# Decay and beta columns carried by the neighbourhood values' weights, values early and gates late

## The chip, the cores and the metric

The kernel runs on one core of one Trainium2 chip. The metric is the device time of one execution in microseconds (us). Beside it stands one profiled execution, from which all stretches, waits and durations are read. Engines are named as in the profile: PE is the tensor engine (matmuls), PEld its weight load, DVE the vector engine, ACT the scalar engine, POOL the GpSimd engine, and SP the engine whose queue issues nearly all DMA transfers.

## The reference

One layer of a hybrid backbone, on 1024 latent tokens and 256 context tokens of width 1024. Modulation vectors come from `silu(c) @ w_ada`. Tokens are normalised and modulated, and one projection `@ w_in` gives all columns:

```python
px = modulate(rms_norm(x, norm1_w[i]), sh1, sc1) @ w_in[i]
pc = modulate(rms_norm(ctx, norm1_w[i]), csh1, csc1) @ w_in[i]
```

- Group A, gated DeltaNet, four heads of 128, forward and backward: q, k, v go through a short convolution and SiLU; `z` (512 columns) gives the output gate `silu(z)`; 16 columns give the decay (`a`) and the strength (`b`) per head and direction. Chunks of tokens need the inverse of a triangular matrix built from k, decay and beta, and then a scan over the chunks with a state per head. The context is scanned first.
- Group B, neighbourhood attention, eight heads of 64: each latent query attends to a window of latent keys and to all context keys.

Both outputs go through one projection, a gated residual, and a SwiGLU feed-forward. Only the latent stream is returned, so the gate `z` is needed for the 1024 latent tokens alone, the decay and beta columns and the values of group B for all 1280.

## The kernel before, in words

Tokens are cut into ten tiles of 128 (two of context, eight latent). The normalised input is held transposed in eight K-slices as a pair of rounded parts, `hh` and `hl`; each weight is split in the same way by ACT (rounded part) and POOL (remainder), and each product is three matmuls per K-slice (line 389 for blocks, line 572 for wide jobs).

The projection is a list `jobs`, run in order by the loop over `n`:

- A `Block` computes 128 columns for all tokens with the weight stationary, in segments of 256, 512 and 512 tokens. Kinds are k, q, v (convolution and SiLU behind it) and nk, nq (keys and queries of group B, with their norm). Its `evac`, `silu`, `norm` and `finish` come in the following jobs.
- A `Wide` job computes half of z or half of group B's values (nv) with the tokens stationary, one tile at a time, 24 matmuls per tile. Its weights come in two loads of 132 columns (z) or 128 (nv). The 16 decay and beta columns stand at the end of z's weights: z's second half computes 248 columns of z and these 16, and, for the two context tiles, only these 16. They go to the tile `ab`.

The order before is: k0, k1, k2, k3, z second half, nk0 to nk2, z first half, nk3, nq0 to nq2, q0 to q3, nv first half, v0, nv second half, v1, v2, v3, nq3.

Beside the jobs run background generators, a few steps per tile or per K-slice: the modulation of the later parts (`modulation`, weights `wad`), then, from the job after the fifth on, `block_inverses` and `preps`. `block_inverses` starts from `ab` (`decay_tables`), runs a long chain on DVE (lines 825 and 827), transposes the result on PE (line 837) and stores it as `x_d`. `preps` makes, for each chunk and direction, a corrected matrix: it loads `kk`, `xc` and, for latent chunks, `at` (lines 872 to 877), takes an Exp on ACT (line 901), matmuls on PE (lines 897 to 920) with sums on DVE (lines 903 and 921), and stores `at_d` and `y_d` (line 930). The latent chunks start only when all q blocks are done. A wide job steps the background by 2 per tile before `turn` and by 5 behind it, a block by 1 and by 3 per K-slice.

All values of a half are stored to memory (`nv_d`); behind the job numbered `values`, sixteen copies from memory to memory (line 1024) cut them into the windows' blocks (`vw_d`). When all `preps` are done, `attention` starts its loads on SP, and behind the last block the scan starts, with the attention as its filling.

The order in which each engine's queue gets its instructions is made by a planner from the program's order and its own estimate of durations; each engine then works strictly in that order. SP's queue is in order too: a transfer that waits holds all that stand behind it. Buffers come from rings: two for `zt` (wide results on their way to memory), three shared under the tag `kx` (kTh, kk, kd, vt, hl16), three for `at`, four banks of PSUM for `blk` behind the fifth job, eight before.

Of the kernel before, what the change touches and what calls it, by code (L numbers as in the profile page):

```python
# [9 lines left out]
F32 = mybir.dt.float32  # L10
# [3 lines left out]
AF = mybir.ActivationFunctionType  # L14
# [22 lines left out]
def const_arrays():  # L37
    p = np.arange(128)[:, None]
    f = np.arange(128)[None, :]
    same = (p // 32) == (f // 32)  # L40
    m = [p == f, p <= f, p >= f, p > f, p < f, (p > f) & same, (p < f) & same]
    big = np.stack([x.astype(np.float32) for x in m[:3] + [(p // 64) == (f // 64)]], 1)
    f32 = np.arange(32)[None, :]
    q = p % 32
    small = np.stack([x.astype(np.float32) for x in
                      [q <= f32, q >= f32, q < f32, q > f32]], 1)
    out = np.concatenate([big.reshape(128, -1), small.reshape(128, -1)], 1)
    masks = np.stack([x.astype(np.float32) for x in m[3:]], 1)
    return np.ascontiguousarray(out), np.ascontiguousarray(masks)
# [38 lines left out]
def hybrid(ctx, tc, a, dbg):  # L88
    nc = tc.nc
    pe, act, dve, pool, sp = nc.tensor, nc.scalar, nc.vector, nc.gpsimd, nc.sync  # L90

    def pools(stack, name, side=None, bufs=1, **kw):
        if side:
            kw["side"] = side
        return stack.enter_context(tc.tile_pool(name=name, bufs=bufs, reuse_waits="tile", **kw))
# [19 lines left out]
    def const(name, shape, dt=F32):  # L115
        return mid.tile(shape, dt, name=name, tag=name)
# [26 lines left out]
    z_d = dram.tile([L, 512], F32, name="z_d", tag="z_d")  # L143
# [4 lines left out]
    nv_d = dram.tile([T, 512], F32, name="nv_d", tag="nv_d")  # L148
# [14 lines left out]
    ab = const("ab", [128, NCH, 16])  # L163
# [196 lines left out]
    with ExitStack() as bs:  # L360
# [7 lines left out]
        def bank(name="m"):  # L368

            if len(psum) == 1:  # L370
                return psum[0].tile([128, 512], F32, name=name, tag="ps")
            return psum[1].tile([128, 512], F32, name=name, tag=name, bufs=4 if name == "blk" else 2)
# [19 lines left out]
        class Block:  # L392


            def __init__(self, kind, i):
                self.kind, self.i = kind, i
                self.segs = SEGS[1:] if kind in ("q", "nq") else SEGS
                self.t0 = self.segs[0][0]
# [149 lines left out]
        class Wide:  # L548


            def __init__(self, kind, half, zp):
                self.kind, self.half, self.zp = kind, half, zp
                self.n = 264 if kind == "z" else 256

            def prefetch(self):
                h2, n = 2 * self.half, self.n // 2
# [19 lines left out]
            def tiles(self):  # L576
                half = self.half
                if self.kind == "nv":
                    for t in range(NCH):
                        p = self.wide(t, 0, 256)  # L580
                        vt = cp.tile([128, 264], F32, name="zt", tag="zt", bufs=2)
                        act.copy(vt[:, :256], p[:, :256])
                        sp.dma_start(nv_d[t * 128:(t + 1) * 128, half * 256:half * 256 + 256], vt[:, :256])
                        yield
                    return
                if half == 1:
                    for t in range(2):
                        p = self.wide(t, 248, 264)
                        act.copy(ab[:, t], p[:, :16])
                    yield  # L590
                nz = 264 if half == 0 else 248
                for t in range(2, NCH):
                    p = self.wide(t, 0, 264)
                    zt = cp.tile([128, 264], F32, name="zt", tag="zt", bufs=2)
                    act.activation(zt[:, :nz], p[:, :nz], AF.Silu)
                    if half:
                        act.copy(ab[:, t], p[:, 248:264])
                    sp.dma_start(z_d[(t - 2) * 128:(t - 1) * 128, half * 264:half * 264 + nz], zt[:, :nz])
                    yield


        first = [Block("k", 0), Block("k", 1)]
        with ExitStack() as xs:
# [67 lines left out]
            for s0, n in SEGS:  # L671
                p = bank()
# [7 lines left out]
            for k in range(KT):  # L680
# [3 lines left out]
                t = xt[k]  # L684
# [16 lines left out]
        cp = pools(bs, "cp", "right")  # L701
# [248 lines left out]
                    live = nxt  # L950
                flush(tick[0] + 2)

        jobs = first + [Block("k", 2), Block("k", 3), Wide("z", 1, zp)]
        inv = len(jobs)
        jobs += [Block("nk", i) for i in range(3)] + [Wide("z", 0, zp), Block("nk", 3)]
        jobs += [Block("nq", i) for i in range(3)] + [Block("q", 0)]
        turn = len(jobs)
        jobs += [Block("q", i) for i in (1, 2, 3)]
        later = len(jobs)
        values = later + 2  # L960
        queries = range(turn - 1, later)
        jobs += [Wide("nv", 0, zp), Block("v", 0), Wide("nv", 1, zp), Block("v", 1), Block("v", 2), Block("v", 3), Block("nq", 3)]

        def blk(n):
            return jobs[n] if 0 <= n < len(jobs) and isinstance(jobs[n], Block) else None
# [351 lines left out]
    with ExitStack() as os_:  # L1317
# [25 lines left out]
        for b in range(KT - 2):  # L1343
            w, nxt = nxt, load_w(a["w_out"][b + 1], lo_engine=dve)
# [38 lines left out]
    with ExitStack() as us:  # L1383
# [66 lines left out]
        for f in range(PLAIN):  # L1450
            po = [[bank(), bank()] for _ in range(2)]
            g = prev[f]
            w = [up.next(), None]
# [103 lines left out]
    for n, (wn, xn) in enumerate(zip(Stream.DOWN, FACTORS)):  # L1557
        o = chains[n in (1, 3, 5)]
        for p in range(NFB // 2):
            w = up.next(1)[0]  # L1560
# [19 lines left out]
def host(inputs):  # L1580
    f = lambda n: np.asarray(inputs[n])
    c = np.ascontiguousarray
    o = {}
    o["cst"], o["masks"] = const_arrays()
    o["c2"] = c(np.stack([f("c")[0].reshape(8, 128), f("c_ctx").reshape(8, 128)], -1).transpose(1, 0, 2))
    o["prm"] = c(np.concatenate([f("norm1_w")[0].reshape(8, 128), f("norm2_w")[0].reshape(8, 128),
                                 f("b_ada")[0].reshape(48, 128)], 0).T)
    o["cw"] = c(f("dn_conv_w")[0].reshape(5, 12, 128).transpose(2, 1, 0))
    o["qkw"] = c(np.stack([np.tile(f("na_q_norm_w")[0], 2), np.tile(f("na_k_norm_w")[0], 2)], -1))
    o["onw"] = c(f("dn_out_norm_w").reshape(128, 1))  # L1590
    o["adt"] = c(np.concatenate([f("dn_A_log")[0].reshape(1, 8), f("dn_dt_bias")[0].reshape(1, 8)], 1))
    xc = np.concatenate([f("ctx")[0], f("x")[0]], 0)
    o["xcT"] = c(xc.T.reshape(8, 128, T))
    wada = f("w_ada")[0]
    o["wa1"] = c(wada[:, :2048].reshape(8, 128, 4, 512).transpose(2, 1, 0, 3)[[2, 0, 3, 1]])
    o["wa2"] = c(wada[:, 2048:].reshape(8, 128, 8, 512).transpose(2, 1, 0, 3))
    w = f("w_in")[0]

    def blocks(w, n=128):
        return c(w.reshape(w.shape[0] // 128, 128, w.shape[1] // n, n).transpose(2, 1, 0, 3))  # L1600

    o["w_conv"] = blocks(w[:, :1536])
    o["w_z"] = blocks(w[:, 1536:2064], 132)
    o["w_nqk"] = blocks(w[:, 2064:3088])
    o["w_nv"] = blocks(w[:, 3088:3600])
    o["w_out"] = blocks(f("w_out")[0])
    gu = np.stack(np.split(blocks(f("w_ffn_in")[0]), 2, 0), 1)
    o["w_gu"] = c(gu.reshape(NFB, 2, 128, 2, 4, 128).transpose(0, 1, 3, 2, 4, 5))
    fo = blocks(f("w_ffn_out")[0]).reshape(2, 4, 128, NFB // 2, 2, 128)
    o["w_fo"] = c(fo.transpose(3, 0, 4, 2, 1, 5))  # L1610
    tab = np.concatenate([f("na_rpb")[0].reshape(8, 465), np.full((8, 1), -1.0e30, np.float32)], 1)
    o["rpb"] = c(tab[:, bias_index()])
    return o


def bias_index():

    idx = np.empty((2, 3, 128, 384), np.int64)
    pad = 15 * 31
    for half in range(2):  # L1620
        for case, cb in enumerate((0, 1, 3)):
            q = np.arange(128)
            r, cq = (half * 8 + q // 16)[:, None], (cb * 16 + q % 16)[:, None]
            k = np.arange(384)
            kr, kc = (half * 4 + k // 32)[None, :], (BLKS[cb] + k % 32)[None, :]
            r0 = np.clip(r - 4, 0, 8)
            w0 = np.clip(cq - 8, 0, 48)
# [19 lines left out]
```

## Time and profile before

| what | value |
|---|---|
| runs | 1632.72, 1635.08, 1635.48 us (median 1635.08) |
| profiled execution | span 1634.2 us; a time of its own beside the span is not given |
| PE busy | 1525.4 us (93%) |
| DVE busy | 1037.2 us (63%) |
| ACT busy | 705.7 us (43%) |
| POOL busy | 203.0 us (12%) |
| traffic | 275.23 MB, 168 GB/s on the mean of the span |
| granted clock of PE, mean | 0.971 |

In rows of windows, each engine's busy time and its count of instructions stand first, then the granted clock (PEclk, 1.00 is full), the busy share of the sixteen DMA engines, and GB/s. In rows of the timeline: start, duration, engine, line, operation, tile written and tiles read, shapes, and in brackets the idle time before it with what ended it. In rows of waits: who waited, for whom, us in total, times, longest. `1.00` as a DMA share means that all engines are busy. A busy PE may run at half its clock.

### The profile page before, as it was taken

How to read it: one execution, taken by the hardware profiler on the slowest of the kernel's cores; microseconds unless marked ns; L12 is line 12 of the kernel's file. 1: busy time of each engine (PE TensorE's matmuls, PEld its weight loads, DVE VectorE, ACT ScalarE, POOL GpSimd, SP SyncE). 2: the span in 40 equal slices, each digit the busy share in tenths (PEclk: the TensorE clock that was granted, in tenths of full speed). 3: DMA queues.
4: the chain of work that ended last, by engine and by line, in shares of the span. 5: the costliest groups of instructions: out<-in, count | busy, mean ns of one | idle time of the engine just before them, and what ended most of it. 6: DMA issues, size and time to landing. Idle time of an engine off the chain costs nothing.

```text
span 1634.2 us, 24148 instructions
## 1 busy us (share of the span) xinstructions
PE 1525.4 (93%) x8642; PEld 1284.3 (79%) x8642; DVE 1037.2 (63%) x1934; ACT 705.7 (43%) x1340; POOL 203.0 (12%) x275
## 2 busy tenths in 40 slices
PE   3999999999988798999998999999999999999999
PEld 1689787779888786878776787888888888888887
DVE  5855678444364466567898538966565666679752
ACT  5342363663332234565665228433333333445441
POOL 2053611522333220000010000000000000000000
PEclk9998999999999899999998999999999999999999
DMA  9366121535345527999954920532322333798752
GB/s 371 122 195 190 56 75 41 185 120 187 110 131 169 197 93 198 311 276 288 269 175 144 301 102 33 168 123 97 104 97 97 100 107 108 227 364 293 269 162 84
DMA packets 211720, 275.23 MB, mean 168 GB/s; under 512 B 16144, under 2 KB 120080, under 8 KB 210576
## 3 DMA queue, kind: packets, MB, share of 16 engines
q1 hardware_dynamic: 210736, 273.06, 51.6%
q8 instruction: 68, 1.11, 0.3%
q10 hardware_dynamic: 864, 0.63, 0.1%
q14 instruction: 52, 0.43, 0.1%
HBM read 206.78 MB, written 71.04 MB: 170 GB/s over the span
## 4 chain that ended last, share of the span: by engine, by line
PE 64%; DMA 5%; DVE 5%; ACT 3%; issue 2%; SPq 1%; POOL 0%; DVEq 0%; ACTq 0%
PE ps L1219 25%; PE ps L1566 13%; PE blk L389 4%; PE ps L1350 3%; PE blk L572 3%; PE pr L920 2%; PE sc L317 2%; DMA at_d<-at 2%; PE sc L307 2%; PE sc L295 2%; PE ps L1112 1%; DVE cacc L445 1%; PE ps L1372 1%; PE ps L1124 1%; PE pr L911 1%
## 5 line engine op out<-in xcount | busy, mean ns | idle before, releaser
L389 PE MATMUL blk<-hh,whi 128*128 128x512 f32 (+1 forms) x416 | 126.6, 398 | 3.4 <-ACT whi L198 1.6
L389 PE MATMUL blk<-hh,wlo 128*128 128x512 f32 (+1 forms) x416 | 120.4, 383 | 2.3 <-POOL wlo L199 2.3
L1280 ACT CAST uhi<-ws 128x512 fp32r<-128x512 f32 x91 | 54.8, 623 | 151.4 <-PE ps L1219 72.8
L1280 ACT CAST uhi<-wq 128x512 fp32r<-128x512 f32 x101 | 60.6, 621 | 134.9 <-issue 61.6
L389 PE MATMUL blk<-hl,whi 128*128 128x512 f32 (+1 forms) x416 | 117.3, 380 | 0.0
L1281 DVE TENSOR_TENSOR ulo<-wq,uhi 128x512 fp32r<-128x512 f32 x101 | 67.5, 688 | 66.3 <-ACT uhi L1280 36.1
L1219 PE MATMUL ps<-hT,uhi 128*128 128x512 f32 x336 | 104.1, 391 | 3.1 <-ACT hT L1398 3.1
L1219 PE MATMUL ps<-lT,uhi 128*128 128x512 f32 x336 | 104.0, 391 | 0.0
L1219 PE MATMUL ps<-hT,ulo 128*128 128x512 f32 x336 | 103.5, 389 | 0.0
L572 PE MATMUL blk<-zhi,hh 128*128 128x256 f32 (+2 forms) x304 | 90.8, 299 | 0.0
L389 PEld LDWEIGHTS blk<-hh,wlo 128*128 128x128 f32 x416 | 75.2, 196 | 19.2 <-POOL wlo L199 2.8
L1219 PE MATMUL ps<-hB,uhi 128*128 128x512 f32 x288 | 89.7, 392 | 0.0
L1219 PE MATMUL ps<-lB,uhi 128*128 128x512 f32 x288 | 89.3, 391 | 0.0
L1219 PE MATMUL ps<-hB,ulo 128*128 128x512 f32 x288 | 88.8, 389 | 0.0
L572 PE MATMUL blk<-zhi,hl 128*128 128x256 f32 (+2 forms) x304 | 88.4, 291 | 0.0
L572 PE MATMUL blk<-zlo,hh 128*128 128x256 f32 (+2 forms) x304 | 87.9, 289 | 0.0
L389 PEld LDWEIGHTS blk<-hh,whi 128*128 128x128 f32 x416 | 72.7, 198 | 18.4 <-issue 3.6
L389 PEld LDWEIGHTS blk<-hl,whi 128*128 128x128 f32 x416 | 75.0, 196 | 14.1 <-DVE hl L690 0.3
L1281 DVE TENSOR_TENSOR ulo<-ws,uhi 128x512 fp32r<-128x512 f32 x91 | 60.8, 687 | 37.6 <-ACT uhi L1280 29.3
L903 DVE SCALAR_TENSOR_TENSOR kk<-kk,NB,y 128x128 f32<-128x128 f32 x80 | 37.8, 529 | 62.5 <-ACT y L901 62.5
L198 ACT CAST whi<-wraw 128x1024 fp32r<-128x1024 f32 x26 | 27.3, 1049 | 116.0 <-PE blk L389 48.8
L1219 PEld LDWEIGHTS ps<-hT,uhi 128*128 128x128 f32 x336 | 63.0, 188 | 16.3 <-ACT hT L1398 3.5
(333 smaller groups left out, 3778.3 us busy)
## 6 DMA issues: line engine op xcount, KB each, us to landing
wq<-w_fo SPq DMA_DIRECT2D x99, 256.0 KB
wq<-w_gu SPq DMA_DIRECT2D x88, 256.0 KB
wad<-wa SPq DMA_DIRECT2D x64, 256.0 KB
bt<-rpb SPq DMA_DIRECT2D x64, 192.0 KB
t_d<-g SPq DMA_DIRECT2D x22, 512.0 KB
fr<-t_d SPq DMA_DIRECT2D x44, 256.0 KB
f_d<-g SPq DMA_DIRECT2D x33, 256.0 KB
fr<-f_d SPq DMA_DIRECT2D x33, 256.0 KB
```

Source lines behind the costliest of these rows:

```text
L295: pe.matmul(sc[:, u * 640 + n0:u * 640 + n1], q, ks[i], start=i == 0, stop=i == 1)
L307: pe.transpose(sc[:, u * 640 + j * 128:u * 640 + (j + 1) * 128], bt[:, j * 128:(j + 1) * 128], ident)
L317: pe.matmul(sc[u * ND:u * ND + ND, 1280:1408], vv, pt[:, j * 128:(j + 1) * 128], start=j == 0, stop=j == 4)
L389: pe.matmul(o, ww[:, k], xx[k][:, s], start=k == 0 and j == 0, stop=k == KT - 1 and j == end)
L572: pe.matmul(p[:, :c1 - c0], x[k][:, s], ww[:, k, c0:c1], start=k == 0 and j == 0, stop=k == KT - 1 and j == 2)
L903: dve.scalar_tensor_tensor(kk[:, h], kk[:, h], NB[:, d, c, h:h + 1], e[:, h], op0=OP.mult, op1=OP.mult)
L920: pe.matmul(p[:, hs[h]], f[:, h], src[:, h], start=True, stop=True)
L1219: pe.matmul(o, w[wi][:, k], x[xi][:, k], start=first and k == 0 and j == 0, stop=k == n - 1 and j == 2, skip_group_check=True)
L1280: act.copy(hi, self.raw[key])
L1281: dve.tensor_tensor(lo, self.raw[key], hi.bitcast(F32), OP.subtract)
L1350: pe.matmul(o, w[wi][:, k], parts[xi][k][:, s], start=k == 0 and j == 0, stop=k == KT - 1 and j == 2)
L1566: pe.matmul(o[b], w[wi][:, b], F[xn, p][xi], start=n in (0, 1, 5) and p == 0 and j == 0, stop=p == NFB // 2 - 1 and j == 2, skip_group_che ...
```

## The change

The 16 decay and beta columns move from the end of z's weights to the end of the values' weights (in the host's arrangement and in `tiles`). The values' halves take the places of z's halves in the list, the fifth and the ninth job, and z's halves take theirs, the eighteenth and the twentieth. The values' second half computes 248 values and the 16 columns for all ten tiles; there is no tile any more that computes the 16 columns alone. The copies into `vw_d` follow the values' first half, the ninth job. A gate tile is copied to one of four places of a `kx` buffer; after four tiles one Silu runs over all four in place and one transfer stores them. z's weights are loaded in blocks of 128 columns, the values' in blocks of 132.

```diff
-                self.n = 264 if kind == "z" else 256
+                self.n = 256 if kind == "z" else 264
...
                 if self.kind == "nv":
+                    nv = 248 if half else 264
                     for t in range(NCH):
-                        p = self.wide(t, 0, 256)
+                        p = self.wide(t, 0, 264)
                         vt = cp.tile([128, 264], F32, name="zt", tag="zt", bufs=2)
-                        act.copy(vt[:, :256], p[:, :256])
-                        sp.dma_start(nv_d[t * 128:(t + 1) * 128, half * 256:half * 256 + 256], vt[:, :256])
+                        act.copy(vt[:, :nv], p[:, :nv])
+                        if half:
+                            act.copy(ab[:, t], p[:, 248:264])
+                        sp.dma_start(nv_d[t * 128:(t + 1) * 128, half * 264:half * 264 + nv], vt[:, :nv])
                         yield
                     return
-                if half == 1:
-                    for t in range(2):
-                        p = self.wide(t, 248, 264)
-                        act.copy(ab[:, t], p[:, :16])
-                    yield
-                nz = 264 if half == 0 else 248
                 for t in range(2, NCH):
-                    p = self.wide(t, 0, 264)
-                    zt = cp.tile([128, 264], F32, name="zt", tag="zt", bufs=2)
-                    act.activation(zt[:, :nz], p[:, :nz], AF.Silu)
-                    if half:
-                        act.copy(ab[:, t], p[:, 248:264])
-                    sp.dma_start(z_d[(t - 2) * 128:(t - 1) * 128, half * 264:half * 264 + nz], zt[:, :nz])
+                    p = self.wide(t, 0, 256)
+                    if t % 4 == 2:
+                        zt = cp.tile([128, 4, 256], F32, name="z4", tag="kx", bufs=3)
+                    act.copy(zt[:, (t - 2) % 4], p[:, :256])
+                    if t % 4 == 1:
+                        act.activation(zt, zt, AF.Silu)
+                        sp.dma_start(z_d[(t - 5) * 128:(t - 1) * 128, half * 256:half * 256 + 256]
+                                     .rearrange("(c p) d -> p c d", p=128), zt)
                     yield
...
-        jobs = first + [Block("k", 2), Block("k", 3), Wide("z", 1, zp)]
+        jobs = first + [Block("k", 2), Block("k", 3), Wide("nv", 1, zp)]
         inv = len(jobs)
-        jobs += [Block("nk", i) for i in range(3)] + [Wide("z", 0, zp), Block("nk", 3)]
+        jobs += [Block("nk", i) for i in range(3)] + [Wide("nv", 0, zp), Block("nk", 3)]
...
-        values = later + 2
+        values = inv + 3
...
-        jobs += [Wide("nv", 0, zp), Block("v", 0), Wide("nv", 1, zp), Block("v", 1), ...]
+        jobs += [Wide("z", 0, zp), Block("v", 0), Wide("z", 1, zp), Block("v", 1), ...]
...
-    o["w_z"] = blocks(w[:, 1536:2064], 132)
+    o["w_z"] = blocks(w[:, 1536:2048])
...
-    o["w_nv"] = blocks(w[:, 3088:3600])
+    o["w_nv"] = blocks(np.concatenate([w[:, 3088:3600], w[:, 2048:2064]], 1), 132)
```

More of the change, by code (lines that the diff above doesn't have):

```diff
@@ L959, in hybrid @@
         later = len(jobs)
-        values = later + 2
+        values = inv + 3
         queries = range(turn - 1, later)
-        jobs += [Wide("nv", 0, zp), Block("v", 0), Wide("nv", 1, zp), Block("v", 1), Block("v", 2), Block("v", 3), Block("nq", 3)]
+        jobs += [Wide("z", 0, zp), Block("v", 0), Wide("z", 1, zp), Block("v", 1), Block("v", 2), Block("v", 3), Block("nq", 3)]
         def blk(n):
```

## The prediction

> **What bounds the kernel now.** I read the page first, then the busy time in short windows, then the waits of the tensor engine (PE) and of SP's DMA queue, then the timeline where those pointed. The page:
>
> ```profile
> span 1634.2 us, 24148 instructions
> PE 1525.4 (93%) x8642; PEld 1284.3 (79%) x8642; DVE 1037.2 (63%) x1934; ACT 705.7 (43%) x1340; POOL 203.0 (12%) x275
> PE 64%; DMA 5%; DVE 5%; ACT 3%; issue 2%; SPq 1%; POOL 0%; DVEq 0%; ACTq 0%
> ```
>
> PE is busy 93% of the span and holds 64% of the chain that ended last. So time is won in three ways only: PE work taken away, PE work done at a higher granted clock, or PE idle time closed. All jobs that the change touches lie between 113 and 640 us, so I looked there for each of the three.
>
> The gates' second half (z1, the fifth job) begins with two context tiles that compute only the 16 decay and beta columns. Four windows of that job (busy time of PE, PEld, DVE, ACT, POOL, then granted clock, DMA share, GB/s), the first and last of the narrow matmuls, and the first wide one:
>
> ```profile
> 113.86:116.20 2.34, 2.34 (x24) 2.34 (x22) 0.00 (x0) 0.00 (x0) 0.00 (x0) 1.00 1.05 327
> 116.20:121.96 5.76, 5.76 (x29) 5.76 (x29) 3.46 (x7) 3.40 (x7) 4.35 (x2) 0.51 0.67 225
> 121.96:130.00 8.04, 8.04 (x38) 8.04 (x39) 7.75 (x12) 0.76 (x2) 4.02 (x9) 0.50 0.44 136
> 130.00:158.40 28.40, 28.40 (x241) 28.24 (x239) 11.43 (x12) 8.29 (x25) 7.02 (x9) 1.00 0.69 211
> ...
> 113.89 0.26 PE L572 MATMUL blk<-zhi,hh 128*128 128x16 f32 x1
> ...
> 121.75 0.36 PE L572 MATMUL blk<-zlo,hh 128*128 128x16 f32 x1
> ...
> 124.43 0.57 PE L572 MATMUL blk<-zhi,hh 128*128 128x264 f32 x1
> ```
>
> The busy column calls all four windows full. The clock does not: it falls to 0.5 some 2.3 us after the narrow matmuls begin and comes back only at 130.0, 8 us after the last of them.
>
> The second place is the inverse of the decay blocks, which is VectorE's (DVE's) work:
>
> ```profile
> 272.00:276.00 4.00, 3.60 (x16) 2.64 (x15) 3.83 (x6) 0.00 (x0) 0.00 (x0) 1.00 0.00 1
> 276.00:280.00 4.00, 0.93 (x5) 0.78 (x6) 3.57 (x9) 0.00 (x0) 0.00 (x0) 1.00 0.00 0
> 280.00:284.00 4.00, 4.00 (x22) 3.46 (x21) 0.00 (x0) 2.76 (x6) 2.28 (x1) 0.57 0.00 0
> ...
> PE m L837 <- DVE N L831: 3.5, 1, 3.5
> ```
>
> PE has run out of work and waits for the finished inverse, then pays 4 us at clock 0.57.
>
> The third is late, while the blocks' corrections (`preps`) run beside the neighbourhood values and the v blocks:
>
> ```profile
> 525.00:530.00 5.00, 0.92 (x8) 0.71 (x7) 0.00 (x0) 0.00 (x0) 1.59 (x2) 0.93 0.63 179
> 530.00:535.00 5.00, 3.50 (x13) 3.24 (x14) 1.74 (x5) 1.58 (x4) 1.55 (x2) 0.50 1.02 335
> 535.00:540.00 5.00, 4.96 (x36) 4.67 (x35) 2.43 (x6) 2.91 (x8) 0.91 (x2) 0.89 0.67 194
> ...
> 560.00:565.00 5.00, 3.49 (x22) 2.89 (x20) 0.21 (x1) 0.88 (x2) 2.04 (x2) 1.00 0.35 127
> 565.00:570.00 5.00, 0.00 (x0) 0.00 (x0) 0.00 (x0) 0.17 (x1) 0.00 (x0) 0.68 0.87 290
> 570.00:575.00 5.00, 4.14 (x15) 3.75 (x16) 2.34 (x6) 3.08 (x9) 0.00 (x0) 0.50 0.62 212
> 575.00:580.00 5.00, 5.00 (x29) 4.45 (x28) 2.01 (x5) 0.60 (x1) 2.04 (x2) 0.79 0.24 86
> ...
> SPq L877 <- DMA at_d<-at: 43.3, 10, 8.1
> ```
>
> Every engine stands still here, so it is a transfer that is late. SP issues in order; its load of the next `at` (L877) waits until an earlier `at` has been stored (three buffers), 43.3 us in all, and everything behind it in SP's queue waits too. How long such a store takes, by SP's timeline and by the chain of waits, and when the copies into `vw_d` run:
>
> ```profile
> 481.14 0.32 SPq L930 DMA_DIRECT2D at_d<-at  x1
> 483.15 0.32 SPq L877 DMA_DIRECT2D at<-qk_d  x1
> ...
> 517.08 9.42 DMA at_d<-at
> 540.23 10.88 DMA at_d<-at
> 554.12 10.39 DMA at_d<-at
> ...
> L1024 SPq DMA_DIRECT2D vw_d<-nv_d x16: 590/614/852, 498.6 to 554.6; - x16
> ```
>
> Alone, store and wait are over in 2.0 us. While the sixteen copies from memory to memory (L1024, 498.6 to 554.6) are under way they take 9.4 to 10.9 us. Both long stalls of PE lie behind them.
>
> **The change part by part.**
>
> *Narrow matmuls.* The 16 columns now ride in the last 16 of the values' 264, whose job visits all ten tiles anyway, so the 48 matmuls of 16 columns go. They and the transposes that follow them stand from 113.86 to 121.96 us: 8.1 us. Bounds: 48 matmuls at the unthrottled pace of the first window (2.34 us for some 22) are 5.2 us, and 8.1 is what they took. I take 8.1, since it is the measured stretch.
>
> *The half clock after them.* From 121.96 to 130.00 PE worked 8.04 us at 0.50. At full clock that is 4.0 us less, if nothing else throttles there; bounds 0 and 4.0, I take 4.0, since a full clock goes with dense 264-wide work in the fourth window.
> The Trainium skill (TensorE: Matmul & The Clock Gate, Part 1) says that the clock rises after a busy window of about 3.4 us. The wide matmuls began at 124.4 and the clock came back at 130.0, 5.6 us later, so the row is longer than the page; by the page this term would be 2.9 us, an estimate from (124.4 + 3.4 − 121.96) / 2.
>
> *Columns.* Twenty values tiles grow by 8 columns and sixteen gate tiles shrink by 8. The pace of each width, from rows 24 and 20 matmuls apart:
>
> ```profile
> 227.00 0.28 PE L572 MATMUL blk<-zhi,hh 128*128 128x264 f32 x1
> ...
> 229.92 0.28 PE L572 MATMUL blk<-zhi,hh 128*128 128x264 f32 x1
> ...
> 395.64 0.28 PE L572 MATMUL blk<-zhi,hh 128*128 128x256 f32 x1
> ...
> 398.01 0.28 PE L572 MATMUL blk<-zlo,hh 128*128 128x256 f32 x1
> ```
>
> 2.92 / 24 = 121.7 ns and 2.37 / 20 = 118.5 ns, so 480 × 3.2 − 384 × 3.2 ns = +0.3 us.
>
> *Four tiles move from late to early.* Ten tiles instead of eight in the fifth and the ninth job: each early job gets 2 × 2.92 = 5.8 us, and the late ones lose 4 × 24 × 0.1185 = 11.4 us. On a PE that is full in both places this is worth nothing. But the ninth job lies just ahead of the inverse's end. The inverse starts as much earlier as the fifth job ends earlier (it needs the decay columns), DVE's own time for it stays, and PE reaches L837 5.8 us later relative to it; the idle 0.40 + 3.07 = 3.5 us is then filled, and with it goes 0.43 × 4 = 1.7 us lost to the clock behind the gap. Bounds 0 and 5.2; I take 4.
>
> *The copies into `vw_d` go early*, behind the ninth job (the rows at 227 us lie in its first two tiles, and seven more of 2.92 us end near 250) instead of behind the last values. Sixteen issues of 0.614 us (9.8 us of SP) and their traffic leave the late stage. What they may hit now is SP's next load of weights and the stores of the inverses behind it:
>
> ```profile
> 260.00:264.00 4.00, 4.00 (x22) 3.39 (x21) 3.88 (x4) 0.00 (x0) 0.00 (x0) 1.00 0.00 0
> ...
> 268.40 0.59 SPq L197 DMA_DIRECT2D wraw<-w_nqk  x1
> ...
> 280.11 1.05 ACT L198 CAST whi<-wraw 128x1024 fp32r<-128x1024 f32 x1 [11.65 <-PE blk L389]
> ```
>
> The DMA engines are idle there (share 0.00), SP has nothing to issue until 268.4, and the weights loaded then are converted only at 280.1, when PE frees their buffer. That cover hides them: 0. Late, the two stalls are 4.08 + 1.50 = 5.6 and 1.51 + 5.00 + 0.86 = 7.4 us, and the clock after them costs 0.50 × 3.50 + 0.11 × 4.96 + 0.50 × 4.14 + 0.21 × 5 = 5.4 us: 18.4 in all. Bounds 0 (the three buffers alone cause them) and 18.4. I take 13, nearer the top, because a store without the copies took 2.0 us.
>
> *Stores and Silu of the gates.* Sixteen Silus from PSUM become sixteen copies, and four Silus over 128x1024; sixteen stores of z become four. The nearest rows, all of 390 to 645 us:
>
> ```profile
> L582 ACT COPY zt<-blk 128x256 f32<-128x256 f32 x20 | 7.4, 371 | 55.1 <-PE blk L572 37.5 <-DMA nv_d<-zt 10.5 <-issue 6.6
> L901 ACT ACT_TABLE_LOAD x3 | 3.8, 1283 | 0.1
> L452 ACT ACTIVATE cacc<-cacc 128x1024 f32<-128x1024 f32 x2 | 2.1, 1060 | 1.1 <-DVE cacc L445 1.1
> ```
>
> A late gate tile costs ACT the same 0.37 us as a values tile did. New are four Silus of 1.06 us, and for each up to two table loads, since the corrections' Exp (L901) stands around them: 4 × (1.06 + 2 × 1.28) = 14.5 us at most on an engine that is mostly idle. In exchange ACT no longer waits 10.5 us for the stores of two small buffers. The new tile takes one of three `kx` buffers for four tiles, beside q2's and q3's kTh and kk; the fifth tile's copy may wait for the first store (512 KB), ACT's and not PE's wait, since four PSUM banks lie between.
>
> *What gets worse.* The wide jobs step the corrections five at a time per tile, so 4 × 5 = 20 of their 112 late steps fall into the v blocks (three per k), and the corrections end nearer to the last block. Behind their end stand the attention's loads on SP:
>
> ```profile
> 607.43 0.32 SPq L930 DMA_DIRECT2D y_d<-y  x1
> ...
> 650.10 0.56 SPq L1066 DMA_DIRECT2D kT<-kT_d  x1
> ```
>
> Of the PE work inside those 42.7 us, 20 / 3 steps of k, each 9 matmuls at the 0.17 us of the last late window (29 in 5 us), come to lie ahead of the corrections' end: 10 us of cover less. Also the first corrections meet a wide job that is two tiles, 48 × 0.1185 = 5.7 us, shorter. No row prices this; bounds 0 and 16 (both fully exposed), I take 5, since three quarters of the 42.7 us remain as cover.
>
> **Sum**: −8.1 − 4.0 + 0.3 − 4 − 13 + 5 = −23.8 us. The execution's span is 1634.2; the runs lie between 1632.72 and 1635.48 around 1635.08, so what lies around the span is about 0.9 us and the profile is an ordinary run. 1634.2 − 23.8 + 0.9 = **1611.3 us**.
>
> **Rivals.**
> 1. *Only the PE work goes* (stalls stay). For it: L877 waits also before the first copy (483.15), so the `at` ring may be the cause. Against: 2.0 against 10 us per store. −8.1 − 4.0 + 0.3 = −11.8: 1623.
> 2. *All stalls close and nothing new comes*: −8.1 − 4.0 + 0.3 − 5.2 − 18.4 = −35.4: 1600. For it: both stalls follow the copies, and all other work is only moved. Against: a new order has seldom no wait of its own, and ACT's queue gets longer work.
> 3. *Silu among Exp.* If every Silu with its two table loads lands on the corrections' chain (Exp waits on ACT, DVE on Exp, PE's L911 on DVE), 14.5 us come back in place of the 5: 1621. For it: Silu and Exp share one engine that works in order. Against: ACT has 10.5 us less to wait.
> The Trainium skill (ScalarE: Activation LUTs, Table sets) tells one to group activations by table set, and it speaks against this move, since late the gates' Silu stands between two Exp; the trace agrees that a load costs 1283 ns.
> 4. *Slower: the copies stand in front of the early weights.* Place: behind the ninth job. They read and write 16 × 0.26 MB each way, 8.4 MB; at 170 GB/s, the mean of the span, 49 us, so from 252 to 301 us. The weights of 268.4 would land after 301 instead of before 280.1, 21 us late, and PE would stand and then run cold (some 3 us). With the late stalls kept by the `at` ring: 1635 − 12 + 24 = 1647. It decides once the copies are still under way 12 us after 280. Against: the second window of the late fence moved 335 GB/s with these copies in it, at which 8.4 MB are 25 us and end before 280.
>
> **How the numbers follow.** Forecast 0.46, rival 1 0.18, rival 2 0.19, rival 3 0.08, rival 4 0.09. The forecast's own range is 1604 to 1619. The range 1597 to 1631 takes in rivals 1, 2 and 3 and leaves out rival 4 and the tails. A change below 0.2% (3.3 us) can't be told from none. Faster 0.87: the first four, less 0.04 for cases of rivals 1 and 3 in which the late stage loses another 10 us; same 0.04; slower 0.09.
>
> **What would show it.** Right: no 128x16 matmul; clock 1.0 from 114 to 150; the fifth job ending some 6 us earlier; no wait of PE at L837; the L1024 issues near 250 us; `at_d` stores of 2 to 4 us throughout; no window of 5 us without PE between 500 and 600. Wrong: a wait of the early casts on `wraw`; waits of L911 as long as before; PE idle at the start of the attention; waits of PE on q3's kTh.

## The result and the profile after

The changed kernel takes 1608.62 us (median, 1606.48 to 1609.03) against 1633.9 us of the kernel before on the same chip: a ratio of 0.9852, 95% interval 0.9836 to 0.9869, 25.3 us less. The profiled executions differ by 1634.2 − 1606.5 = 27.7 us. The forecast was 1611.3 us and the range 1597 to 1631: the time came out as said, but several terms of its sum did not.

The head of the page of the kernel after, and its chain's shares by engine. Lines of the code from about 600 on stand one lower than before (L1024 is now L1023, L877 is L876, L930 is L929, L837 is L836).

```profile
span 1606.5 us, 24016 instructions
PE 1504.8 (94%) x8594; PEld 1265.4 (79%) x8594; DVE 1037.5 (65%) x1934; ACT 713.9 (44%) x1348; POOL 201.2 (13%) x275
PE 75%; DVE 7%; DMA 7%; ACT 5%; issue 3%; POOL 2%; SPq 1%; ACTq 0%; DVEq 0%; POOLq 0%
```

PE is busy 20.6 us less; 48 matmuls are gone (8642 to 8594). PE holds 75% of the chain in place of 64%. Where the time goes is read from the same five points of both executions: the last copy of decay columns (end of the fifth job), the first matmul behind the ninth job, PE's wait for the inverse, the first copy of the first late wide job, and the last matmuls of the last block. Before:

```profile
158.24 0.17 ACT L597 COPY ab<-blk 128x16 f32<-128x16 f32 x1
...
251.12 0.74 PE L389 MATMUL blk<-hh,whi 128*128 128x256 f32 x3
...
279.07 0.45 PE L837 MATMUL m<-cst,N 80*128 80x80 f32 x2 [3.47 <-DVE N L831]
279.32 0.71 PE L389 MATMUL blk<-hl,whi 128*128 128x512 f32 x2
...
398.33 0.37 ACT L582 COPY zt<-blk 128x256 f32<-128x256 f32 x1 [3.79 <-PE blk L572]
...
635.53 0.62 PE L389 MATMUL blk<-hh,wlo 128*128 128x512 f32 x2
```

After:

```profile
153.31 0.18 ACT L585 COPY ab<-blk 128x16 f32<-128x16 f32 x1
...
250.79 0.74 PE L389 MATMUL blk<-hh,whi 128*128 128x256 f32 x3
...
272.54 0.53 PE L836 MATMUL m<-cst,N 80*128 80x80 f32 x2 [3.16 <-DVE N L830]
272.80 1.20 PE L389 MATMUL blk<-hh,whi 128*128 128x512 f32 x2
...
398.28 0.37 ACT L593 COPY z<-blk 128x256 f32<-128x256 f32 x1 [3.79 <-PE blk L572]
...
607.70 0.63 PE L389 MATMUL blk<-hh,wlo 128*128 128x512 f32 x2
```

| stretch | moved point | four tiles' work in it | by equal work |
|---|---|---|---|
| to the end of the fifth job | −4.9 us | +5.8 | −10.7 |
| to the first late wide copy | −0.05 | 96 × 0.1217 = +11.7 | −11.7 |
| from there to the last block's last matmuls | −27.8 | −11.4 | −16.4 |
| from there to the end | 998.7 and 998.8: +0.1 | 0 | +0.1 |

So the early part won 11.7 us, all of it by the end of the fifth job but 1 us, and the late part won 16.4. The forecast had 15.8 (8.1 + 4.0 − 0.3 + 4) and 8 (13 − 5). The split is known to some 2 or 3 us only: a second profiled execution of the kernel after (the one run beside the kernels with both late loads put back, below) has its first late wide copy at 400.07 and the last matmuls at 606.86, which gives −10.0 early and −19.0 late.

The fifth job's windows, at the times of the prediction's fence:

```profile
113.86:130.00 16.14, 16.14 (x137) 16.14 (x137) 11.21 (x18) 7.19 (x17) 8.47 (x10) 1.00 0.66 208
130.00:150.00 20.00, 20.00 (x171) 20.00 (x170) 10.49 (x11) 4.77 (x16) 6.67 (x9) 1.00 0.83 264
```

No stretch at half clock is left. The late windows, the wait for `at` in SP's queue, one store of `at_d` with the next load behind it, and the copies into `vw_d`:

```profile
520.00:540.00 20.00, 19.22 (x129) 17.04 (x129) 9.02 (x16) 5.26 (x13) 5.70 (x15) 1.00 0.46 150
540.00:560.00 20.00, 17.20 (x92) 14.61 (x90) 16.70 (x23) 9.88 (x19) 8.86 (x7) 0.91 0.22 75
560.00:580.00 20.00, 17.29 (x120) 15.21 (x120) 14.20 (x25) 5.36 (x8) 4.52 (x9) 1.00 0.18 66
...
SPq L876 <- DMA at_d<-at: 17.5, 8, 3.9
...
520.72 0.32 SPq L929 DMA_DIRECT2D at_d<-at  x1
523.08 0.32 SPq L876 DMA_DIRECT2D at<-qk_d  x1
...
L1023 SPq DMA_DIRECT2D vw_d<-nv_d x16: 590/643/2442, 232.4 to 268.3; - x16
```

The copies are issued from 232 to 268 us. A store of `at_d` and the wait behind it now take 2.4 us, the waits are 17.5 us in place of 43.3, and no window is nearly empty.

### The profile page after: what moved, and what is told of

Its sections match the earlier page's. It is cut to its first block, busy times and chain, and to the rows that moved or that the text cites. A ratio compares the mean times of both kernels' runs of the same rounds, so it can differ in the third digit from the quotient of the medians.

```text
span 1606.5 us, 24016 instructions
## 1 busy us (share of the span) xinstructions
PE 1504.8 (94%) x8594; PEld 1265.4 (79%) x8594; DVE 1037.5 (65%) x1934; ACT 713.9 (44%) x1348; POOL 201.2 (13%) x275
## 4 chain that ended last, share of the span: by engine, by line
PE 75%; DVE 7%; DMA 7%; ACT 5%; issue 3%; POOL 2%; SPq 1%; ACTq 0%; DVEq 0%; POOLq 0%
PE ps L1218 26%; PE ps L1565 13%; PE blk L389 10%; PE ps L1349 3%; PE blk L572 3%; PE pr L919 3%; PE sc L317 3%; PE sc L307 2%; PE sc L295 2%; PE pr L910 1%; PE ps L1111 1%; DVE tt L824 1%; PE ps L1371 1%; DMA nv_d<-zt 1%; DMA fraw<-w_conv 1%
## 5 line engine op out<-in xcount | busy, mean ns | idle before, releaser
L572 PE MATMUL blk<-zhi,hh 128*128 128x264 f32 (+1 forms) x288 | 83.9, 291 | 0.0
L572 PE MATMUL blk<-zhi,hl 128*128 128x264 f32 (+1 forms) x288 | 82.1, 285 | 0.0
L572 PE MATMUL blk<-zlo,hh 128*128 128x264 f32 (+1 forms) x288 | 81.7, 284 | 0.0
L1218 PEld LDWEIGHTS ps<-hT,uhi 128*128 128x128 f32 x336 | 63.1, 189 | 16.4 <-ACT hT L1397 3.5
L1218 PEld LDWEIGHTS ps<-lT,uhi 128*128 128x128 f32 x336 | 63.4, 189 | 13.2
```

What stands on the lines that cost most here:

```text
L572: pe.matmul(p[:, :c1 - c0], x[k][:, s], ww[:, k, c0:c1], start=k == 0 and j == 0, stop=k == KT - 1 and j == 2)
L1218: pe.matmul(o, w[wi][:, k], x[xi][:, k], start=first and k == 0 and j == 0, stop=k == n - 1 and j == 2, skip_group_check=True)
```

## The experiments

Times are medians; each ratio is to the kernel before, run beside it on the same chip, so that chips on which the kernel before takes a slightly different time can be set beside each other. All of these kernels compute the whole result.

### The narrow matmuls alone

In the kernel before, the two context tiles of the fifth job are computed at full width.

```diff
-                        p = self.wide(t, 248, 264)
-                        act.copy(ab[:, t], p[:, :16])
+                        p = self.wide(t, 0, 264)
+                        act.copy(ab[:, t], p[:, 248:264])
```

> The kernel before, with the two context tiles of the fifth job computed at full width (264 columns, of which the 16 are copied out) in place of 16 columns. Theory (the narrow matmuls take 8.1 us and pull the clock to 0.5, also for 8 us behind them): the narrow stretch of 8.1 us and the 4.0 us go, 2 x 2.92 us of wide work come: -6.3 us, 1627 to 1629, with the clock at 1.00 from 114 to 150 us. Rival (the clock would fall there anyway, and a narrow matmul costs only its own pace, 5.2 us for 48): 5.8 - 5.2 = +0.6 us and half a clock for some 14 us as before: 1634 or more.

Measured: 1626.34 us against 1633.38, ratio 0.9954 (0.9939 to 0.9968), −7.0 us. Its window:

```profile
113.86:130.00 16.14, 16.14 (x138) 16.14 (x137) 11.05 (x18) 7.83 (x19) 8.46 (x10) 1.00 0.62 198
```

Sixteen times as many columns for two tiles made the kernel faster, and the half clock is gone with nothing else edited. The narrow matmuls cause it, and 8.1 + 4.0 us is their price within the interval of this ratio.

### The copies' line moved back

```diff
-        values = inv + 3
+        values = later + 2
```

> The kernel after, with the sixteen copies into vw_d issued behind the second gate job (the place they had before) and nothing else changed. Theory (the copies make the stores of at_d slow, 2 to 10 us, and with them PE stalls): 13 to 18 us slower than after, 1621 to 1627, with stores of at_d of about 10 us beside the copies, an SP wait at L876 of some 40 us and two windows of 5 us nearly without PE. Rival (the three buffers for at alone make the stalls, or the smaller number of stores of z and nv late): within 3 us of after, 1606 to 1612, stores of at_d of 2 to 4 us.

Measured: 1609.12 us against 1633.38, ratio 0.9843 (0.9824 to 0.9862): as the kernel after. But this tells nothing of the theory, since the copies did not go late:

```profile
L1023 SPq DMA_DIRECT2D vw_d<-nv_d x16: 589/647/2442, 233.7 to 270.0; - x16
```

In this run, as in the kernel after, the planner issued the copies when their data was there and not where their line stands. So `values` is an edit without effect here; what brought the copies forward is that the values are early.

### The copies really held back

A corner of 64 × 8 values per group of four copies is written to `nv_d` again, with the same values, from a tile that needs a result of the second gate job; the copies must follow it.

```diff
+                    if half and t % 2:
+                        i = (t - 3) // 2
+                        act.activation(late0[:, i:i + 1], p[:, 0:1], AF.Copy, scale=0.0)
+                        act.activation(kept[:, i], keep[:, i], AF.Identity, bias=late0[:, i:i + 1])
+                        sp.dma_start(nv_d[CT + i * 256:CT + i * 256 + 64, 0:8], kept[0:64, i])
...
```

> The line at which the copies into vw_d stand does not decide when they go: the run before this one had them early again, since the planner issues a transfer as soon as its data is there. Here they are tied to late data: one 64 x 8 corner of nv_d per group of four copies is written again, with the same values, from a tile that needs a result of the second gate job, and the four copies come behind it, between 470 and 560 us as in the kernel before. Theory (the copies slow the stores of at_d, and with them come the late stalls): 13 to 18 us slower than after, 1621 to 1627, stores of at_d of about 10 us beside the copies. Rival (what counts is that late no value tile is stored any more, 20 stores of 128 KB in SP's queue and ACT's waits for them): within 4 us of after, 1605 to 1613.

Measured: 1617.34 us against 1633.08, ratio 0.9907 (0.9887 to 0.9927); the kernel after has 0.9852 (0.9836 to 0.9869). That is 9 us slower by the ratios. The place where it stalls (in this kernel L606 is the copy, L942 the stores, L889 the load of `at`):

```profile
510.98 2.84 SPq L606 DMA_DIRECT2D vw_d<-nv_d  x4
513.86 2.21 SPq L942 DMA_DIRECT2D at_d<-at  x1
...
524.97 0.32 SPq L889 DMA_DIRECT2D at<-qk_d  x1
...
520.00:530.00 10.00, 3.35 (x16) 2.82 (x15) 2.34 (x6) 2.02 (x5) 0.71 (x1) 0.69 0.55 174
...
SPq L889 <- DMA at_d<-at: 44.6, 9, 7.8
```

Four copies, a store of `at_d` right behind them, and 11.1 us until the next load may go. The waits are 44.6 us, as before the change (43.3), and PE stands 6.65 us in one window. Holding the copies back adds little of its own: they wait 6.0 us in SP's queue for the corners (420 to 600 us), and in the kernel before they waited 6.4 us for the values' stores. The mechanism of the prediction holds; its price of 13 us does not, since 9 lies between the 4 of the rival and the 13 to 18 of the theory.

### A store for each gate tile

The gates' Silu and store per tile through the two `zt` buffers, as they were before the change; the copies stay early.

```diff
-                        zt = cp.tile([128, 4, 256], F32, name="z4", tag="kx", bufs=3)
...
+                    zt = cp.tile([128, 264], F32, name="zt", tag="zt", bufs=2)
+                    act.activation(zt[:, :256], p[:, :256], AF.Silu)
+                    sp.dma_start(z_d[(t - 2) * 128:(t - 1) * 128, half * 256:half * 256 + 256], zt[:, :256])
```

> The kernel after with Silu and a store of its own for each gate tile through the two zt buffers, as the gates had them in the kernel before: 16 stores of 128 KB late in place of four of 512 KB. Theory of the copies: within 4 us of after, 1605 to 1613. Rival (the many small stores and ACT's waits for them made the late stalls): 10 to 16 us slower, 1618 to 1625, with PE windows of 5 us nearly empty between 490 and 560.

Measured: 1613.27 us against 1633.08, ratio 0.9883 (0.9861 to 0.9905), 5 us slower than after by the ratios (the intervals just overlap). Between the two expectations, and again neither. SP's waits for the wide results between 420 and 600 us are 11.6 us in eight waits in this kernel and 2.2 us in three in the kernel after: a store in SP's queue waits for ACT's result, and the corrections' loads wait behind it.

That these waits are the 5 us is not shown, though. The first gate tile and the last matmuls of the last block in this kernel:

```profile
402.35 0.38 ACT L592 ACTIVATE zt<-blk 128x256 f32<-128x256 f32 x1 [3.79 <-PE blk L572]
...
612.22 0.63 PE L389 MATMUL blk<-hh,wlo 128*128 128x512 f32 x2
```

Between them lie 209.9 us, against 209.4 and 206.8 in the two executions of the kernel after. This execution is 3.9 us longer than the first of these, but it is already 4.1 us behind at the first gate tile, ahead of everything that was edited, and 2.7 us behind at the first matmul of the fifth job (116.05 against 113.36). So in the profile the stores cost between 0.5 and 3 us where they stand, no more than executions of one kernel differ there.

### Silu per tile, one store for four

```diff
-                    act.copy(zt[:, (t - 2) % 4], p[:, :256])
+                    act.activation(zt[:, (t - 2) % 4], p[:, :256], AF.Silu)
                     if t % 4 == 1:
-                        act.activation(zt, zt, AF.Silu)
```

> The kernel after, with Silu per gate tile straight from PSUM (16 Silus of about 0.4 us into the four places, no copies, one store for four as before). Theory (ACT has cover late, and table loads lie beside PE's work): within 3 us of after, 1606 to 1612, though the table loads between 390 and 615 us rise from 12 to 20 or more. Rival (each Silu among the corrections' Exp lies on their chain): every added pair of loads costs 2.6 us, 10 to 20 us slower, 1618 to 1629, with PE waits for ACT y L900 in the list of waits.

Measured: 1610.54 us against 1633.38, ratio 0.9855 (0.9834 to 0.9875): as after. The table loads of the gates and the corrections' Exp between 390 and 615 us, in this kernel:

```profile
L899 ACT ACT_TABLE_LOAD x8 | 10.3, 1283 | 0.1
L593 ACT ACT_TABLE_LOAD x5 | 6.4, 1283 | 0.1
```

In the kernel after there are 5 and 2. Six more loads, 7.7 us of ACT, cost nothing that can be told from none. The stretch from the first gate tile (402.29) to the last matmuls of the last block (612.00) is 209.7 us, the same as with a store per tile. So the stage does not show what sets the two medians apart (1610.54 and 1613.27, with intervals that overlap), and a price of the store alone is not shown.

### Both late loads put back

The two edits above together: copies held back, Silu and store per tile. With it on the same chip the kernel after, unchanged.

> The kernel after with both late loads of the kernel before put back: the copies held back by late data as in the run with the held copies, and a Silu and a store of its own for each gate tile. Theory (the late gain, 27.9 us less the 11.4 us of moved tiles, that is 16.5 us, is these two: 8.7 and 4.7 us alone): 13 to 18 us slower than after, 1621 to 1627. Rival (the two overlap, and the rest of the late gain comes from elsewhere): the larger of the two alone, 1616 to 1619.

> The kernel after, unchanged, on the same chip as the two that follow, as their measure: 1606 to 1610.

Measured: 1623.46 us, ratio 0.9940 (0.9923 to 0.9957), against 1606.9 us, ratio 0.9850 (0.9832 to 0.9868), for the kernel after beside it: 16.6 us by the medians, 14.7 by the ratios. The late part had won 16.4. Two windows and the wait in this kernel:

```profile
520.00:530.00 10.00, 5.42 (x33) 4.39 (x31) 2.61 (x5) 1.19 (x3) 4.02 (x5) 0.90 0.48 166
530.00:540.00 10.00, 5.65 (x27) 5.14 (x28) 3.12 (x7) 3.84 (x10) 2.00 (x2) 0.59 0.69 215
...
SPq L885 <- DMA at_d<-at: 48.2, 10, 8.8
```

The picture of the kernel before is back, a PE half idle for 20 us and the clock at 0.59 in the second ten, although all other parts of the change are in. The totals look like a proof that the late gain is these two loads; the stage says less. The same two points in the kernel with the held copies and in this one:

```profile
399.80 0.37 ACT L598 COPY z<-blk 128x256 f32<-128x256 f32 x1 [3.79 <-PE blk L575]
...
617.85 0.62 PE L392 MATMUL blk<-hh,wlo 128*128 128x512 f32 x2
```

```profile
403.36 0.38 ACT L597 ACTIVATE zt<-blk 128x256 f32<-128x256 f32 x1 [3.78 <-PE blk L575]
...
622.14 0.63 PE L392 MATMUL blk<-hh,wlo 128*128 128x512 f32 x2
```

The last two columns are PE's busy and idle time between the two points:

| kernel | first late wide tile | last block's last matmuls | between | busy | idle |
|---|---|---|---|---|---|
| before | 398.33 | 635.53 | 237.2 | 214.3 | 22.9 |
| before, less the four tiles | | | 225.8 | 202.9 | 22.9 |
| after | 398.28 | 607.70 | 209.4 | 197.4 | 12.0 |
| after, beside this kernel | 400.07 | 606.86 | 206.8 | 195.7 | 11.1 |
| a store for each gate tile | 402.35 | 612.22 | 209.9 | 194.2 | 15.6 |
| copies held back | 399.80 | 617.85 | 218.1 | 197.4 | 20.6 |
| both late loads | 403.36 | 622.14 | 218.8 | 197.3 | 21.5 |

The copies lengthen the stretch by 8.6 us (11.3 against the other execution), all of it idle time of PE. Both loads lengthen it by 9.4 (12.0), less than 1 us more than the copies alone. The profiled spans on this chip are 1621.4 and 1604.6 us, 16.8 apart, and of these 3.3 lie ahead of the first gate tile and 1.5 behind the blocks, where nothing was put back. So the copies are shown, at some 9 us; the stores' share is 0.5 to 3 us. Some 7 us of the late part's 16.4 (225.8 to 218.8) no run here takes back: 5.6 of them are busy time of PE for the same work, 202.9 us at a granted clock of 0.94 before and 197.3 at 0.96 here. Why the clock was lower before is open. Executions of the kernel after differ by 2.6 us in this stretch, so these figures are good to about 3 us.

### Four buffers for `zt`

```diff
-                        vt = cp.tile([128, 264], F32, name="zt", tag="zt", bufs=2)
+                        vt = cp.tile([128, 264], F32, name="zt", tag="zt", bufs=4)
```

> The kernel after, with four buffers for zt in place of two. Theory (ACT's 18 us of waits for nv_d stores in the fifth job, behind the wad loads in SP's queue, delay its other copies: PE waits 1.1 us for kk L534 at 155 us and 1.4 us for cr L477 at 196 us, which the kernel before did not have): the waits for zt go, the fifth job ends 1 to 3 us earlier: 1605 to 1608. Rival (the decay columns come at PE's pace anyway and the planner's order takes up the rest): no change, 1608 to 1610.

Measured: 1607.4 us against 1633.38, ratio 0.9841 (0.9819 to 0.9862). In the kernel after ACT waits 18.0 us for these buffers from 100 to 160 us, in six waits. With four buffers the last copy of the decay columns comes at 151.91 in place of 153.31 us. The wait is real, and it can be the 1.4 us that the fifth job fell short of the forecast. In the time it is 1.2 us, less than can be told from none.

### More background steps in the late gate jobs

```diff
-                        bg.step(5)
+                        bg.step(7)
```

> The kernel after with seven background steps per tile of the late gate jobs in place of five: 16 x 2 = 32 of the corrections' steps go from the v blocks into the gate jobs. Theory of my term of +5 (steps pushed into the v blocks shorten the cover ahead of the attention's loads): the corrections end some 15 us earlier and up to 5 us are won, 1603 to 1607. Rival (the corrections go at the pace of their own chain of stores, Exp and sums, whatever steps they get): no change, 1606 to 1611.

Measured: 1606.01 us against 1633.08, ratio 0.9842 (0.9817 to 0.9868), not to be told from after. But the corrections end much earlier. The last `y_d` store, after:

```profile
584.21 0.32 SPq L929 DMA_DIRECT2D y_d<-y  x1
```

and with seven steps:

```profile
575.06 0.32 SPq L929 DMA_DIRECT2D y_d<-y  x1
```

Nine us earlier for the corrections, 7 for the scan's first load (617.70 in place of 624.85), and by the medians 2.6 us for the whole. Seven and nine steps, both with four `zt` buffers:

> The kernel after with seven background steps per late gate tile and four zt buffers. If the two small gains seen alone (2.6 and 1.2 us) are real and lie in different stages, they add: 3 to 4 us below after, 1604 to 1605.5. If they are scatter: as after within 1.5 us.

> As the one before with nine steps per tile. If the corrections follow the steps given, they end still earlier and the attention's loads find more cover: 1602 to 1605. If seven steps already exhaust their own chain: as with seven, within 1.5 us; if more corrections beside the short gate jobs starve PE there: 2 to 4 us slower than with seven.

Measured, beside 1606.9 us (0.9850) for the kernel after: 1604.56 us, ratio 0.9824 (0.9808 to 0.9840), and 1607.07 us, ratio 0.9838 (0.9818 to 0.9857). Seven steps with four buffers is the fastest that ran, 2.3 us below the kernel after, but its interval still overlaps the other's; nine steps give no more.

### nk3 ahead of the values' first half

```diff
-        jobs += [Block("nk", i) for i in range(3)] + [Wide("nv", 0, zp), Block("nk", 3)]
+        jobs += [Block("nk", i) for i in range(4)] + [Wide("nv", 0, zp)]
```

> The kernel after with nk3 ahead of the values' first half in place of behind it, so that other work stands ahead of the inverse's end (the wide job and the first q and nq blocks in place of nk3). Theory (the planner puts L836 into PE's queue at the point where its own estimate has the inverse finished, some 3 us early, whatever work surrounds it, and the ready matmuls of the next block stand behind it): PE waits at L836 for 3 us again, and the time is within 4 us of after, 1604 to 1611. My prediction's reading (PE has run out of work there, and more work ahead fills the hole): the wait is gone or under 1 us.

Measured: 1629.44 us against 1632.52, ratio 0.9977 (0.9963 to 0.9992): nearly the whole gain is lost, which neither expectation had said. Nearly all of the loss lies ahead of the first gate tile (419.78 in place of 398.28 us). PE's two waits at L836, ACT's waits for the `zt` buffers, then the early copies, the inverse's stores and the next weights in SP's queue, ACT's cast of these weights, and the windows there:

```profile
276.49 0.45 PE L836 MATMUL m<-cst,N 80*128 80x80 f32 x2 [1.70 <-DVE N L830]
...
285.12 1.33 PE L836 MATMUL m<-cst,N 80*128 80x80 f32 x8 [5.86 <-ACT WK L838]
...
ACT zt L583 <- DMA nv_d<-zt: 24.3, 4, 7.7
...
298.45 2.74 SPq L1023 DMA_DIRECT2D vw_d<-nv_d  x4
301.29 2.35 SPq L845 DMA_DIRECT2D x_d<-WK  x2
...
311.92 0.62 SPq L197 DMA_DIRECT2D wraw<-w_conv  x1
...
319.74 1.05 ACT L198 CAST whi<-wraw 128x1024 fp32r<-128x1024 f32 x1 [18.28 <-DMA wraw<-w_conv]
...
310.00:320.00 10.00, 4.76 (x19) 3.20 (x17) 1.51 (x1) 0.26 (x1) 0.00 (x0) 0.91 0.47 173
320.00:330.00 10.00, 3.42 (x8) 2.43 (x9) 1.61 (x2) 9.82 (x16) 8.93 (x13) 0.50 0.85 262
```

One job later, the values' first half and its copies fall together with the end of the inverse, and PE loses time in two places. First the copies hold SP's queue for 29.3 us, waiting for the values' stores that they read, and the next values' stores stand behind them; ACT waits 24.3 us for the two `zt` buffers (3.6 in the kernel after), is late with its copies of the inverse (`WK`), and PE waits 5.86 us for these at L836. Then the copies stand in front of the inverse's stores and of q's weights: ACT waits 18.28 us for the weights, POOL's remainder follows, and PE is idle 5.24 + 6.58 = 11.8 us in 20 and at half clock in the second ten. This is the prediction's fourth rival in kind, and near its price: by the ratios the kernel is 20 us slower than after (0.9977 − 0.9852 of 1633), where the rival had put 24 on the early part. No run holds the copies back in this order, so their share of the 20 us is read from the waits and not tested. In the changed kernel the copies are issued by 268 us, ahead of all that.

## Why the prediction was right, and where it was wrong

- **Narrow matmuls −8.1, half clock −4.0, columns +0.3.** Right. The windows show clock 1.00, the fifth job ends 10.7 us earlier by equal work, and the run with full context tiles gives −7.0 where these terms less the two tiles' 5.8 gave −6.3. The 8.1 us are the narrow matmuls' alone: the transposes that the prediction counts into them begin at 121.96, which leaves the sum as it is. The 1.4 us missing of the 12 fit ACT's wait for two `zt` buffers, which the prediction had not counted in the early job; ten stores there go beside the `wad` loads.
- **Idle before L837 filled, −4.** Wrong. PE waits 3.16 us in place of 3.47. The step that failed is "PE has run out of work": directly behind the waiting transposes stand matmuls of nk3 that run without a wait of their own, in both traces. PE works in the order it was given, and that order changed: from the ninth job's end to the wait PE had 279.07 − 3.47 − 251.12 = 24.5 us of work before, 272.54 − 3.16 − 250.79 = 18.6 us after. The planner put the transposes 5.9 us of work earlier, and the two tiles moved there (5.8 us) could fill nothing. That it always puts them some 3 us too early is not shown: with nk3 first the wait was 1.7 us. Why its estimate is short stays open.
- **The copies' −13, and stores and Silu at nothing.** The sign and the mechanism of the copies were right, the size wasn't: held late, they cost some 9 us. The prediction had read 18.4 from the two stalls and taken 13, because "a store without the copies took 2.0 us"; the stores did get that short, but the time won by it was smaller than the stalls. Why is not shown. Stores and Silu at nothing is not disproved: six more table loads changed no time, and the stores per tile changed the late stretch by 0.5 to 3 us, though SP waits 9.4 us more for ACT with them. The late part still won 16.4 us, so some 7 of it are in no term of the sum and in no run; most of them (5.6) is PE doing the same work in less busy time, and what raised its clock there stays open.
- **What gets worse, +5.** Too dear. The start of the attention did get worse. The two windows of ten in which PE waits there, before:

```profile
640.00:650.00 10.00, 4.42 (x26) 2.74 (x24) 7.39 (x19) 8.19 (x14) 0.27 (x1) 0.77 0.63 165
650.00:660.00 10.00, 9.02 (x84) 7.50 (x84) 3.94 (x12) 5.53 (x14) 1.22 (x4) 0.89 0.91 297
```

and after:

```profile
610.00:620.00 10.00, 4.01 (x21) 2.27 (x22) 5.66 (x15) 8.33 (x12) 0.00 (x0) 0.87 1.00 250
620.00:630.00 10.00, 8.60 (x47) 6.39 (x47) 4.56 (x12) 4.91 (x9) 1.23 (x3) 0.50 0.62 176
```

  PE is idle 6.6 us before and 7.4 after, and loses 2.0 and 4.8 us to the clock (1 minus the clock, by busy time): 3.6 us worse in this stretch. Yet from the last block's last matmuls to the end both take the same (998.7 and 998.8 us), so it is given back later. The run with seven steps agrees that this place is cheap: nine us more of cover bought some 2.6 us by the medians, which can't be told from none.
- **The sum.** −15.8 early came out as −11.7, −8 late as −16.4. The two errors have opposite signs, and the total is right by 4 us in the profile and by 2.7 in the runs partly for that reason. So much of the closeness is luck: some 4 us that the wait at the inverse kept and 4 by which the copies were too dear stand against the 5 that the cover did not cost and the 7 that stay open.
- **The rivals.** The first (only the PE work goes, −11.8) is near what is left with both late loads put back: 0.9940 of the kernel before, 9.8 us less. The second (1600) needed the L836 wait to go and no stall at all; the late windows still have 5.5 us without PE between 540 and 580. The third fell with the Silu per tile. The Trainium skill (ScalarE: Activation LUTs, Table sets) tells one to group activations by table set; here a load took 1283 ns in every row, and leaving them ungrouped, six loads more, cost nothing that can be told from none. The fourth was real and one job away.

## What to carry to other kernels

Look at the clock beside the busy time: matmuls of 16 columns counted as full work, and computing all 264 columns was faster. Price a transfer by what stands behind it in its queue, and test where the planner really issues it before reading anything from a line that was moved. When a kernel with two loads put back takes as long as the sum of the two alone, compare the stage in which they stand too: here the totals agreed, and the stage gave only one of the two. When copies are moved early, look for what is issued next behind them; here one job's difference in the order took back nearly all of the gain.

## What the runs showed of the hardware

A store of `at_d` (128 x 512 values) and the wait for its end take 2.4 us in the kernel after, and 11.1 us when four copies from memory to memory were issued just ahead of it on the same queue. The window of exactly that store and wait, and the end of it alone, in the run with held copies (granted clock, DMA share and GB/s last), and a stretch of the kernel after in which the copies are under way:

```profile
513.86:524.97 11.11, 6.84 (x41) 5.61 (x39) 3.09 (x5) 1.89 (x4) 5.27 (x8) 0.95 0.42 155
521.00:524.97 3.97, 0.00 (x0) 0.00 (x0) 0.00 (x0) 0.00 (x0) 0.00 (x0) 0.86 0.26 102
...
260.00:270.00 10.00, 9.38 (x44) 7.20 (x42) 9.69 (x10) 3.58 (x5) 2.53 (x1) 1.00 0.26 102
```

The sixteen engines are busy 0.42 of the time on their mean, but that does not say that each of them had room. While the copies are under way the share stands at 0.26 and the traffic at 102 GB/s, in both kernels. 0.26 of sixteen is about four engines, an estimate from these rows: they fit copies that keep four engines full and leave the others idle, and a store that waits for its part on those four. No view shows the engines one by one, so this is not shown. Either way the copies are slow: 102 GB/s is well under the 170 and 335 that the prediction's fourth rival weighed. The Trainium skill (DMA: Bandwidth & Descriptors, Queues, rings and completion order) says that the transfers of one issuing engine share one ring on each DMA engine and are taken in ring order. The rows agree with that; the same copies on another queue were not tried, so it isn't shown here.
